# A token factor that moves behind the MLP's ReLU, one pass over the second half of the output projection, and seven-product up blocks throughout

## The chip, the cores and the metric

The kernel runs on one core of a Trainium2 chip. The metric is the device time of one execution in microseconds; the kernel before takes 2443.19 us as the median of three runs (2441.78 to 2445.8). In the text PE is TensorE, DVE is VectorE, ACT is ScalarE, POOL is GpSimd and SP is SyncE, which issues most of the DMAs.

## What is computed

One layer of a hybrid decoder for 512 prompt tokens and 8 x 4 sample tokens, so 544 columns, model width 2048, MLP width 8192. All of it is fp32. The part that matters here is the second half of the layer:

```
x = x + concat(y_conv, y_delta) @ w_out
h = x * rsqrt(mean(x * x, axis=-1) + EPS) * norm_ffn_w
x = x + square(relu(h @ w_up)) @ w_down
y = rms_norm(x, final_norm_w)
```

The norm has a weight for each of the 2048 features (`norm_ffn_w`) and a factor for each token (the rsqrt). The token factor is positive and the same for all features, so it can be multiplied in before the product with `w_up` or behind it and behind the ReLU.

## The kernel before

**Tiling.** Features lie on the 128 partitions, tokens on the free axis, as two token halves of 272 columns (256 prompt, 16 sample). `x2p` holds x as 8 pair tiles, each of 2 feature tiles by 2 token halves by 272. Every fp32 product is made of three reduced-precision (fp32r) matmuls on split operands: high weight by high x, high by low, low by high (`product`, and the inner loop of `bilinear`). A split is two instructions: ACT copies the value to the high part, DVE subtracts that from the value for the low part. For a weight tile that is `weight` (L142 on ACT, L145 on DVE, 1024 columns, behind a 512 KB load into one of two `w_raw` buffers); for an operand it is `parts_into` (L989 and L990). High and low weights have three buffers each, and `ahead` prepares weights two steps early.

**Output projection.** The first half, `first_part` over `w_o1`, makes both token halves with each weight, into a two-bank tile `ps_big`. The second half runs over `steps`, first all 16 feature tiles for token half 0, then all 16 for half 1. Each of the 16 `w_o2` weights is thus loaded and split twice and used for 24 matmuls each time, into `ps_small`. Each step adds the result into `x2` on DVE (L916), squares the sum on ACT (L1010), adds the square to `ssq` on POOL (L1014) and, after odd steps, stores half of a pair tile (L1016, POOL's queue). `rstd_rows` turns `ssq` into the token factor `r2`: a matmul with ones, Ln and Exp on ACT, one Newton step on DVE. `normalise` multiplies weight and factor into x (L1001, 32 DVE instructions).

**Up.** The 32 blocks of 256 hidden units are of two kinds. The first `N_PLAIN` = 3 are plain: for each token half, two outputs of two weights by 8 k by 3 matmuls, so 192 matmuls a block, each weight loaded once for each half. They end in a Relu on ACT (L1042) for each output. The other 29 are `Pair` blocks: 2x2 blocks of the weights by 2x2 blocks of x in seven products instead of eight, 7 by 8 k by 3 = 168 matmuls of 272 columns. Products run in `ORDER` = 1, 2, 6, 5, 7, 3, 4. The four weight quarters (`w_q`, a11 to a22) come by SP (L1107) into six buffers `g` and two buffers `xe`, the same space that `x2p` held; product 6 forms s1, a21, a11 and a12 on DVE (L1117 to L1120); then each of the seven is split (L1124 on ACT, L1125 on DVE). The x side of the products, tiles c0, c1, c4, d and their parts, is prepared while the plain blocks run.

**Behind a block.** `block_out` copies products 1, 6, 5 from PSUM on ACT (L1190), adds 2, 7, 3 on DVE (L1196), applies Relu to three quarters after product 3 (L1198, 816 wide) and to the last after 4 (L1192, out of PSUM), and squares all on ACT (L1193, 1088 wide). `keep_sums` forms the sums that the way down needs (L1072 to L1076), splits them (L989, L990) and stores them through POOL's queue (`ucd`). Blocks 0 and 1 are kept in another form (`u0_d`), 2 and 31 are stored as they are (`u_d`).

**Order.** The Tile scheduler orders each engine's instructions by priority; `urgent()` raises it. On an engine the instructions run in that order, and an instruction that waits holds all behind it.

Of the kernel before, what the change touches and what calls it, by code (L numbers as in the profile page):

```python
# [9 lines left out]
F32 = mybir.dt.float32  # L10
# [29 lines left out]
N_PLAIN = 3  # L40
# [17 lines left out]
def trunk(ctx, tc, a):  # L58
# [112 lines left out]
    def rstd_rows(out, ssqs, t, halves=(0, 1)):  # L171

        for h in halves:
            pr = ps_small(HT)
            for i, q in enumerate(ssqs):
                PE.matmul(pr, ones, q[:, h, :], start=i == 0, stop=i == len(ssqs) - 1)
            y, th = out[:, h, :], t[:, h, :]
# [772 lines left out]
    sqp = pool("sq", 2, late)  # L950
# [21 lines left out]
    u0_d = [tile_in(dram, f"u0d{m}", [P, 2, 2, 2, HT]) for m in KEPT]
    uc_d = {m: tile_in(dram, f"ucd{m}", [P, 14, HT]) for m in range(N_PLAIN, NF - 1)}
# [11 lines left out]
    def halves_of(t):  # L985
        return t[:, 0, :], t[:, 1, :]

    def parts_into(hi, lo, src):
        S.activation(hi, src, AF.Copy)  # L989
        V.tensor_tensor(lo, src, hi.bitcast(F32), SUB)  # L990


    ssq = t_tile("ssq2", "hi")[:, 0:2]
    r2 = r1
    N2 = KT - N1
    h_c = [{} for _ in range(KT // 2)]

    def normalise(i, h):
        for j in range(2):
            o = 2 * i + j  # L1000
            V.scalar_tensor_tensor(x2[o][:, h], x2[o][:, h], nv[:, KT + o : KT + o + 1], r2[:, h], MUL, MUL)  # L1001

    steps = [(h, o) for h in range(2) for o in range(KT)]
    for (h, ob), w in ahead(steps, lambda it: weight(a["w_o2"][it[1]], N2 * P)):
        ps = ps_small(HT)
        for k in range(N2):
            product({h: ps}, w, k * P, cat[N1 + k], k == 0, k == N2 - 1, (h,))
        add(x2[ob][:, h], ps)
        sq = tile_in(sqp, "sq", [P, HT])
        S.activation(sq, x2[ob][:, h], AF.Square)  # L1010
        if ob == 0:
            G.tensor_copy(ssq[:, h, :], sq)
        else:
            (G if ob < KT - 2 else V).tensor_tensor(ssq[:, h, :], ssq[:, h, :], sq, ADD)  # L1014
# [12 lines left out]

    d_c = [None] * (KT // 2)

    def plain(m, h):  # L1030
        t = t_tile("u", "u")
        u = t[:, :2]
        for i in range(2):
            ps = ps_small(HT)
            for j in range(2):
                with urgent():
                    w = weight(a["w_up"][m, 2 * i + j], 1024)
                for k in range(KT // 2):
                    x = h_c[k][1 + j] if h == 0 else (d_c[k][0][:, j], d_c[k][1][:, j])
                    product({h: ps}, w, k * P, tuple((t, t) for t in x), j == k == 0, j == 1 and k == 7, (h,))  # L1040
            with urgent():
                S.activation(u[:, i], ps, AF.Relu)  # L1042
        with urgent():
            S.activation(u, u, AF.Square)
        if m not in KEPT:
            for i in range(2):
                nc.gpsimd.dma_start(u_d[m][:, 2 * i + 1 - h], u[:, i])
            return
        hi = t[:, 2:4].bitcast(F32R)
        parts_into(hi, u.bitcast(F32R), u)  # L1050
        for i in range(2):
            nc.gpsimd.dma_start(u0_d[m][:, 0, i, h], t[:, 2 + i])
            nc.gpsimd.dma_start(u0_d[m][:, 1, i, h], u[:, i])

    plain(0, 0)
    with urgent():
        rstd_rows(r2, [ssq], t_tile("rt", "T")[:, 0:2], (1,))
    for m in range(1, N_PLAIN):
        plain(m, 0)
    for i in range(KT // 2):  # L1060
        normalise(i, 1)
        p = cmb if i < 7 else cmb2
        d_c[i] = c_tile(p, "d_hi"), c_tile(p, "d_lo")
        parts_into(*d_c[i], x2p[i][:, :, 1, :])
        h_c[i][3] = d_c[i][0][:, 1], d_c[i][1][:, 1]
    for m in range(N_PLAIN):
        plain(m, 1)


    def sums(t, b11, b12, b21, b22, third=True):  # L1070

        V.tensor_tensor(t[:, 1, :], b12, b11, SUB)  # L1072
# [5 lines left out]
    for i in range(KT // 2):
        t = t_tile("tc", ("T", "hi")[i % 2])
        sums(t, *(x2p[i][:, j, h, :] for j in range(2) for h in range(2)), third=False)  # L1080
        hi, lo = c_tile(hlp, "c1_hi"), c_tile(hlp, "c1_lo")
        parts_into(hi, lo, t[:, 0:2, :])
        h_c[i].update({6: (hi[:, 0], lo[:, 0]), 5: (hi[:, 1], lo[:, 1])})
        e = c_tile(cmb2, "c4")
        parts_into(e[:, 0], e[:, 1], t[:, 3, :])
        h_c[i][4] = e[:, 0], e[:, 1]
# [9 lines left out]
    class Pair:  # L1096
# [31 lines left out]
    def bilinear(items, early, cs, outs):  # L1128
# [15 lines left out]
        for (w, p), (whi, wlo) in ahead(items, load):  # L1144
# [39 lines left out]
    def block_out(m):  # L1184
        u = t_tile("u", "u")

        def out(p, ps):
            with urgent():
                if p in (1, 6, 5):
                    S.activation(u[:, {1: 1, 6: 0, 5: 2}[p]], ps, AF.Copy)  # L1190
                elif p == 4:
                    S.activation(u[:, 3], ps, AF.Relu)  # L1192
# [24 lines left out]
    KS = list(range(N_PLAIN, NF - 1))  # L1217
# [274 lines left out]
```

## Time and profile before

| | |
|---|---|
| median of 3 runs | 2443.19 us |
| the profiled execution's own time | 2444.58 us |
| its span in the trace | 2442.8 us |
| PE busy | 2388.2 us |
| DVE busy | 1807.5 us |
| ACT busy | 1080.9 us |
| POOL busy | 495.8 us |
| output projection, second half | 920.6 to about 1023.5 us |
| plain up blocks | to about 1105.6 us |
| seven-product up blocks | to about 1710 us |

The page of the profile gives for each engine the time in which it ran something. Of more use here is the trace by stages: a line of the timeline is start, duration, engine, source line, what is written from what, shape, and in brackets how long the engine had been idle before and what ended that. Differences between starts of the same kind of instruction give the pace of a stage.

### The profile page before, as it was taken

What the parts mean: (1) busy time and instruction counts of PE and PEld (TensorE: products, weight loads), DVE (VectorE), ACT (ScalarE), POOL (GpSimd) and SP (SyncE); (2) the same over time, 40 slices, a digit from 0 to 9 for tenths busy, and PEclk for the clock granted to TensorE, in tenths of its full rate; (3) what the DMA queues carried; (4) which work ended last, traced back from release to release, by engine and by line L of the source; (5) the groups of instructions that cost most, each with busy time, mean ns of one, the idle gap of its engine ahead of it and who ended that gap; (6) DMA issues with size and microseconds to landing.
All of it is one profiled execution on the core that took longest, in us unless ns stands there. A gap on an engine that the chain in (4) does not pass through costs nothing.

```text
span 2442.8 us, 47373 instructions
## 1 busy us (share of the span) xinstructions
PE 2388.2 (98%) x19089; PEld 2362.3 (97%) x19089; DVE 1807.5 (74%) x2937; ACT 1080.9 (44%) x1598; POOL 495.8 (20%) x776
## 2 busy tenths in 40 slices
PE   8999999999999999999999999999899999999997
PEld 8999999999999999998999999999899999999997
DVE  9675575666658535788888888887487788888885
ACT  6424332532432424565555555555233333333445
POOL 5123212312412304410010111110401212121003
PEclk9999999999999999999999999999999999999999
DMA  6233333332423546565555555556945646464433
GB/s 202 93 114 116 98 110 97 122 106 86 134 89 96 173 141 199 199 213 196 194 191 200 200 200 191 189 191 210 375 137 168 226 162 225 154 223 151 143 93 111
DMA packets 144275, 397.96 MB, mean 163 GB/s; under 512 B 35348, under 2 KB 44216, under 8 KB 144056
## 3 DMA queue, kind: packets, MB, share of 16 engines
q1 hardware_dynamic: 108648, 266.12, 34.3%
q0 software_dynamic: 35408, 128.82, 14.2%
q8 instruction: 150, 2.46, 0.4%
q14 instruction: 69, 0.57, 0.1%
HBM read 317.37 MB, written 77.49 MB: 162 GB/s over the span
## 4 chain that ended last, share of the span: by engine, by line
PE 83%; DVE 6%; DMA 6%; issue 2%; ACT 2%; SPq 0%; DVEq 0%; POOLq 0%; POOL 0%; ACTq 0%
PE ps_s L76 46%; PE ps_big L76 29%; PE ps_sm L76 8%; DVE w_lo L145 2%; DMA w_raw<-in_w_o_dram 2%; DMA w_q<-in_w_d_dram 1%; DMA w_raw<-in_w_up_dram 1%; ACT w_hi L142 1%; DVE w_lo L1125 1%; DMA w_q<-in_w_up_dram 1%; DVE x L1001 0%; PE ps_sm L80 0%; DVE yx L799 0%; DMA w_raw<-in_w_d_dram 0%; DMA ud<-u 0%
## 5 line engine op out<-in xcount | busy, mean ns | idle before, releaser
L1124 ACT ACTIVATE w_hi<-w_q 128x768 fp32r<-128x768 f32 (+3 forms) x422 | 375.4, 890 | 555.7 <-PE ps_s L76 496.1
L76 PE MATMUL ps_s<-uc,w_hi 128*128 128x272 f32 x3136 | 592.1, 288 | 5.3 <-DVE x2v L916 4.4
L76 PEld LDWEIGHTS ps_s<-uc,w_hi 128*128 128x128 f32 x3136 | 491.0, 188 | 7.9 <-issue 5.3
L1125 DVE TENSOR_TENSOR w_lo<-w_q,w_hi 128x768 fp32r<-128x768 f32 (+3 forms) x422 | 425.5, 1009 | 59.5 <-ACT w_hi L1124 58.0
L76 PE MATMUL ps_s<-uc,w_lo 128*128 128x272 f32 x1568 | 450.3, 288 | 0.0
L76 PE MATMUL ps_big<-x_hi,w_hi 128*128 128x272 f32 x2016 | 426.4, 293 | 1.3 <-ACT x_hi L157 1.1
L76 PE MATMUL ps_big<-x_hi,w_lo 128*128 128x272 f32 x2016 | 419.3, 289 | 2.6 <-DVE w_lo L145 2.6
L76 PE MATMUL ps_big<-x_lo,w_hi 128*128 128x272 f32 x2016 | 420.2, 289 | 0.3 <-DVE x_lo L160 0.3
L142 ACT ACTIVATE w_hi<-w_raw 128x1024 fp32r<-128x1024 f32 (+3 forms) x215 | 211.4, 983 | 454.0 <-PE ps_big L76 297.6
L145 DVE TENSOR_TENSOR w_lo<-w_raw,w_hi 128x1024 fp32r<-128x1024 f32 (+3 forms) x215 | 279.1, 1298 | 142.0 <-ACT w_hi L142 138.6
L76 PEld LDWEIGHTS ps_big<-x_hi,w_hi 128*128 128x128 f32 x2016 | 317.6, 189 | 5.8 <-ACT x_hi L157 2.3
L76 PEld LDWEIGHTS ps_big<-x_hi,w_lo 128*128 128x128 f32 x2016 | 316.4, 189 | 3.5 <-DVE w_lo L145 3.4
L76 PEld LDWEIGHTS ps_big<-x_lo,w_hi 128*128 128x128 f32 x2016 | 317.7, 189 | 0.7 <-DVE x_lo L160 0.5
L76 PEld LDWEIGHTS ps_s<-uc,w_lo 128*128 128x128 f32 x1568 | 295.0, 188 | 0.0
L76 PE MATMUL ps_s<-c_hi,w_hi 128*128 128x272 f32 x928 | 267.7, 288 | 4.8 <-ACT w_hi L1124 4.2
L76 PE MATMUL ps_s<-c_hi,w_lo 128*128 128x272 f32 x928 | 268.6, 289 | 1.2 <-DVE w_lo L145 0.7
L76 PE MATMUL ps_s<-c_lo,w_hi 128*128 128x272 f32 x928 | 267.6, 288 | 0.0
L1224 POOL DMA_DIRECT2D uc<-ucd x196 | 106.2, 547 | 437.2 <-PE ps_s L76 420.0
L916 DVE TENSOR_TENSOR x2v<-x2v,ps_s 128x272 f32<-128x272 f32 x326 | 140.2, 435 | 66.6 <-PE ps_s L76 64.6
L76 PEld LDWEIGHTS ps_s<-c_hi,w_hi 128*128 128x128 f32 x928 | 175.9, 189 | 5.3 <-ACT w_hi L1124 4.4
L76 PEld LDWEIGHTS ps_s<-c_hi,w_lo 128*128 128x128 f32 x928 | 175.5, 189 | 2.0 <-DVE w_lo L1125 1.0
L76 PEld LDWEIGHTS ps_s<-c_lo,w_hi 128*128 128x128 f32 x928 | 175.5, 189 | 0.0
(375 smaller groups left out, 4224.6 us busy)
## 6 DMA issues: line engine op xcount, KB each, us to landing
w_q<-in_w_up_dram SPq DMA_DIRECT2D x116, 512.0 KB, 4.8
w_raw<-in_w_in_dram SPq DMA_DIRECT2D x106, 512.0 KB, 3.3
uc<-ucd POOLq DMA_DIRECT2D x196, 272.0 KB, 5.7
w_q<-in_w_d_dram SPq DMA_DIRECT2D x128, 384.0 KB, 3.4
w_raw<-in_w_o_dram SPq DMA_DIRECT2D x32, 512.0 KB, 3.4
ucd<-u_hi POOLq DMA_DIRECT2D x28, 544.0 KB, 5.6
ucd<-tc POOLq DMA_DIRECT2D x28, 544.0 KB, 6.7
w_raw<-in_w_up_dram SPq DMA_DIRECT2D x28, 512.0 KB, 3.5
```

The lines of the kernel that those rows point to most:

```text
L76: return cls.held(nc.tensor.matmul(*args, **kw))
L142: S.activation(hi[:, c], raw[:, c], AF.Copy)
L145: V.tensor_tensor(lo[:, c], raw[:, c], hi[:, c].bitcast(F32), SUB)
L916: V.tensor_tensor(out, out, ps, ADD)
L1124: S.activation(hi, s, AF.Copy)
L1125: V.tensor_tensor(lo, s, hi.bitcast(F32), SUB)
L1224: nc.gpsimd.dma_start(t.bitcast(F32), uc_d[KS[j]][:, 2 * b : 2 * b + 2])
```

## The change

- The second half of the output projection runs once over the 16 `w_o2` weights, each with both token halves, 48 matmuls into `ps_big`. Squares, sums and the stores of x are 544 columns or whole pair tiles. The PSUM pool `small2` opens behind it.
- The norm's weight is multiplied in on ACT (`scaled`, 16 instructions kept in program order); the token factor no longer goes into x. `normalise` is gone.
- `operands` prepares c0, d and c4 of pair i-1 in place while the projection works on pair i. The c1 tiles follow behind the last pair, and with them the last readers of the `x2p` space that the quarters use.
- The plain blocks are gone: all 32 blocks take seven products. The first `N_EARLY` = 2 run products 1, 2, 4 of both blocks, with direct weight loads and product 4 in a bank of its own, then 6, 5, 7, 3 of each.
- The token factor is made for both halves after product 4 of block 0.
- `block_out` copies 1, 6, 5 and 4, adds 2, 7, 3, and then `done` runs one DVE instruction over 1088 columns, max with 0 and product with the token factor, ahead of the Square. Both Relus are gone.

```
-    steps = [(h, o) for h in range(2) for o in range(KT)]
-    for (h, ob), w in ahead(steps, lambda it: weight(a["w_o2"][it[1]], N2 * P)):
-        ps = ps_small(HT)
+    def scaled(i):
         for j in range(2):
             o = 2 * i + j
+            tc.keep_in_program_order(
+                S.activation(xs[i][:, j], x2p[i][:, j], AF.Copy, scale=nv[:, KT + o : KT + o + 1])
+            )
+    def operands(i):
+        x = xs[i]
+        b11, b12, b21, b22 = (x[:, j, h, :] for j in range(2) for h in range(2))
+        hi, lo = c_tile(hlp, "c0_hi"), c_tile(hlp, "c0_lo")
+        parts_into(hi, lo, x[:, :, 0, :])
...
+        V.tensor_tensor(b11, b12, b11, SUB)
+        V.tensor_tensor(b12, b22, b12, SUB)
+        V.tensor_tensor(b22, b22, b11, SUB)
+        V.tensor_tensor(b21, b21, b22, SUB)
...
+    for ob, w in ahead(range(KT), lambda o: weight(a["w_o2"][o], N2 * P)):
+        ps = ps_big()
         for k in range(N2):
-            product({h: ps}, w, k * P, cat[N1 + k], k == 0, k == N2 - 1, (h,))
-        add(x2[ob][:, h], ps)
+            product(ps[0], w, k * P, cat[N1 + k], k == 0, k == N2 - 1)
+        add(x2[ob], ps[1])
+        sq = t_tile("sq", "u")[:, 0:2]
+        S.activation(sq, x2[ob], AF.Square)
...
+            nc.gpsimd.dma_start(x2_d[i], x2p[i])
+            if i:
+                scaled(i - 1)
+                operands(i - 1)
     with urgent():
-        rstd_rows(r2, [ssq], t_tile("rt", "T")[:, 0:2], (1,))
...
+        scaled(KT // 2 - 1)
+        operands(KT // 2 - 1)
+        for i in (0, 2, 3, 4, 1, 5, 6, 7):
+            hi, lo = c_tile(hlp, "c1_hi"), c_tile(hlp, "c1_lo")
+            parts_into(hi, lo, xs[i].rearrange("p j h t -> p (j h) t")[:, 0::3])
+            h_c[i].update({5: (hi[:, 0], lo[:, 0]), 6: (hi[:, 1], lo[:, 1])})
...
+        def done():
+            with urgent():
+                V.scalar_tensor_tensor(
+                    u.rearrange("p (i s) t -> p i s t", s=2), u.rearrange("p (i s) t -> p i s t", s=2), 0.0,
+                    r2.unsqueeze(1).broadcast_to([P, 2, 2, HT]), MAX, MUL,
+                )
+                S.activation(u, u, AF.Square)
...
-                if p in (1, 6, 5):
-                    S.activation(u[:, {1: 1, 6: 0, 5: 2}[p]], ps, AF.Copy)
-                elif p == 4:
-                    S.activation(u[:, 3], ps, AF.Relu)
-                    S.activation(u, u, AF.Square)
+                if p in (1, 6, 5, 4):
+                    S.activation(u[:, {1: 1, 6: 0, 5: 2, 4: 3}[p]], ps, AF.Copy)
...
-                if p == 3:
-                    S.activation(u[:, 0:3], u[:, 0:3], AF.Relu)
...
+            if p == 4 and m == 0:
+                with urgent():
+                    rstd_rows(r2, [ssq], hi_t[:, 2:4], swap=True)
...
+    firsts, rest = ups[:N_EARLY], ups[N_EARLY:]
+    items = [(w, p) for w in firsts for p in (1, 2, 4)] + [(w, p) for w in firsts for p in (6, 5, 7, 3)]
+    items += [(w, p) for w in rest for p in ORDER]
+    bilinear(items, firsts, lambda m: h_c, block_out)
```

The diff gives no order of the engines' instructions; three places of it follow. DVE in one steady up block of the kernel before, from the first combination of the quarters (L1117) to the block's split of u; `w_s` is s1, `w_q` a quarter, `u` the block's result, `tc` its sums:

```order
L1117 TENSOR_TENSOR w_s_15654<-w_q 128x1024
L1125 TENSOR_TENSOR w_lo<-w_q,w_hi 128x1024
L1118 TENSOR_TENSOR w_q<-w_q 128x1024
L1120 TENSOR_TENSOR w_q<-w_q 128x1024
L1125 TENSOR_TENSOR w_lo<-w_q,w_hi 128x1024
L1072 TENSOR_TENSOR tc<-u 128x272
L1075 TENSOR_TENSOR tc<-u 128x272
L1073 TENSOR_TENSOR tc<-u,tc 128x272
L1125 TENSOR_TENSOR w_lo<-w_s_15417,w_hi 128x1024
```

The same engine and place in the changed kernel:

```order
L1080 TENSOR_TENSOR w_s_15572<-w_q 128x1024
L1088 TENSOR_TENSOR w_lo<-w_q,w_hi 128x1024
L1081 TENSOR_TENSOR w_q<-w_q 128x1024
L1083 TENSOR_TENSOR w_q<-w_q 128x1024
L1154 SCALAR_TENSOR_TENSOR u<-u,r_91 128x1088
L1088 TENSOR_TENSOR w_lo<-w_q,w_hi 128x1024
L1088 TENSOR_TENSOR w_lo<-w_s_15335,w_hi 128x1024
L1052 TENSOR_TENSOR tc<-u 128x272
```

One instruction of 1088 columns (L1154) now stands between the combinations and the next split, and the sums of u stand one split later; nothing else moved.

ACT at the head of the up stage in the changed kernel, from the last square of the output projection (`sq`); `x2_6`, `xs` are the last two pairs of x, `r1` the token factor:

```order
L1022 ACTIVATE sq_12154<-x2_7_10315 128x544
L994 ACTIVATE x2_6_10313<-x2_6_10313,nv_81 128x544 x2
L978 ACTIVATE c0_hi_12160<-x2_6_10313 128x544
L978 ACTIVATE d_hi_12164<-x2_6_10313 128x272 x2
L179 ACTIVATE r1_91<-ps_sm_12341,eps_t_83 128x272
L179 ACTIVATE r1_91<-ps_sm_12349,eps_t_83 128x272
L180 ACTIVATE r1_91<-r1_91 128x272 x2
L978 ACTIVATE c4_12174<-x2_6_10313 128x272
L994 ACTIVATE xs_11091<-x2_7_10315,nv_81 128x544 x2
L978 ACTIVATE c0_hi_12179<-xs_11091 128x544
L978 ACTIVATE d_hi_12183<-xs_11091 128x272
```

Before, the last pair's operands were split while plain blocks ran; now the scaling and split of the last two pairs, with the token factor's Ln and Exp between them, stand ahead of products 1, 2 and 4 of the first block, which read them.

DVE a little later in the changed kernel, from the split of the last direct weight (`w_lo`, L145) to the split for product 6 of block 0:

```order
L145 TENSOR_TENSOR w_lo_12359<-w_raw_12357,w_hi_12358 128x1024
L979 TENSOR_TENSOR c1_lo_12213<-x2_1_9900,c1_hi_12212 128x544
L979 TENSOR_TENSOR c4_12174<-x2_6_10313,c4_12174 128x272
L979 TENSOR_TENSOR c1_lo_12217<-x2_5_10311,c1_hi_12216 128x544
L1080 TENSOR_TENSOR w_s1_12406<-w_q_12392,w_q_12393 128x1024
L979 TENSOR_TENSOR c1_lo_12221<-x2_6_10313,c1_hi_12220 128x544
L1081 TENSOR_TENSOR w_q_12392<-w_q_12390,w_q_12392 128x1024
L979 TENSOR_TENSOR c1_lo_12225<-xs_11091,c1_hi_12224 128x544
L1082 TENSOR_TENSOR w_q_12390<-w_s1_12406,w_q_12390 128x1024
L1175 TENSOR_TENSOR u_12364<-u_12364,ps_s_12415 128x272
L1083 TENSOR_TENSOR w_q_12391<-w_q_12391,w_q_12390 128x1024
L1088 TENSOR_TENSOR w_lo_12412<-w_q_12390,w_hi_12411 128x1024
```

The c1 splits read the last of the space into which the first quarters are loaded, and they stand among the combinations that wait for those loads; in the kernel before the first combination (L1117 of block 3) stood behind all operand splits, with the plain blocks' matmuls beside them.

More of the change, by code (lines that the diff above doesn't have):

```diff
@@ L169, in product, with rstd_rows @@
                 PE.matmul(ps[h], wp[:, c : c + P], x, start=start and i == 0, stop=stop and i == 2)
-    def rstd_rows(out, ssqs, t, halves=(0, 1)):
+    def rstd_rows(out, ssqs, t, halves=(0, 1), swap=False):
         for h in halves:
@@ L969, in trunk @@
     x2 = [x2p[i // 2][:, i % 2] for i in range(KT)]
+    KS = [m for m in range(NF) if m not in KEPT + STORED]
     x2_d = [tile_in(dram, f"x2d{i}", [P, 2, 2, HT]) for i in range(KT // 2)]
     u_d = {m: tile_in(dram, f"ud{m}", [P, 4, HT]) for m in STORED}
[L972 to L973 removed]
+    u0_d = [tile_in(dram, f"u0d{m}", [P, 2, 4, HT]) for m in KEPT]
+    uc_d = {m: tile_in(dram, f"ucd{m}", [P, 14, HT]) for m in KS}
@@ L975, in trunk, with parts_into @@
     first_part(KT - 1, lambda: None)
     ln_exp(True)
+    def parts_into(hi, lo, src):
+        S.activation(hi, src, AF.Copy)
+        V.tensor_tensor(lo, src, hi.bitcast(F32), SUB)
+    hi_t = t_tile("ssq2", "hi")
+    ssq, r2 = hi_t[:, 0:2], r1
+    N2 = KT - N1
+    h_c = [{} for _ in range(KT // 2)]
+    xs = list(x2p)
+    xs[-1] = t_tile("xs", "T").rearrange("p (j h) t -> p j h t", j=2)
+    def scaled(i):
+        for j in range(2):
+            o = 2 * i + j
+            tc.keep_in_program_order(
+                S.activation(xs[i][:, j], x2p[i][:, j], AF.Copy, scale=nv[:, KT + o : KT + o + 1])
+            )
@@ L983, in bank @@
         return t[:, :HT]
[L985 to L1001, printed above, removed]
@@ L1028, in trunk @@
[L1028 to L1043, printed above, removed]
-            S.activation(u, u, AF.Square)
[L1045 to L1053, printed above, removed]
@@ L1055, in trunk, with sums @@
-    plain(0, 0)
-    with urgent():
-        rstd_rows(r2, [ssq], t_tile("rt", "T")[:, 0:2], (1,))
[L1058 to L1070, printed above, removed]
+    def sums(t, b11, b12, b21, b22):
@@ L1072, in sums @@
         V.tensor_tensor(t[:, 1, :], b12, b11, SUB)
         V.tensor_tensor(t[:, 0, :], b22, t[:, 1, :], SUB)
-        if third:
-            V.tensor_tensor(t[:, 2, :], b22, b12, SUB)
+        V.tensor_tensor(t[:, 2, :], b22, b12, SUB)
         V.tensor_tensor(t[:, 3, :], b21, t[:, 0, :], SUB)
[L1078 to L1086, printed above, removed]
@@ L1110, in parts @@
             n = self.n
-            if p in (1, 2) and self.q is None:
-                return weight(self.src[p - 1], n)
+            if p in (1, 2, 4) and self.q is None:
+                return weight(self.src[{1: 0, 2: 1, 4: 3}[p]], n)
             a11, a12, a21, a22 = self.q
@@ L1149, in bilinear @@
                 w.ps, w.out = {"x": bank(True)}, outs(w.key)
-            if p in (2, 5):
-                w.ps["y" if p == 2 else "z"] = bank(False)
-            ps = w.ps[{2: "y", 5: "z", 3: "z"}.get(p, "x")]
+            alone = p == 4 and w in early
+            if p in (2, 5) or alone:
+                w.ps["z" if p == 5 else "y"] = bank(False)
+            ps = w.ps["y" if alone else {2: "y", 5: "z", 3: "z"}.get(p, "x")]
             c = cs(w.key)
```

78 lines of the change are left out of this document (36 added, 42 removed).

## Prediction

> **What bounds the kernel now.** I read first the busy times and the chain of work that ended last, then windows by stage, then the timelines at the seams of the stages.
>
> ```profile
> PE 2388.2 (98%) x19089; PEld 2362.3 (97%) x19089; DVE 1807.5 (74%) x2937; ACT 1080.9 (44%) x1598; POOL 495.8 (20%) x776
> PE 83%; DVE 6%; DMA 6%; issue 2%; ACT 2%; SPq 0%; DVEq 0%; POOLq 0%; POOL 0%; ACTq 0%
> ```
>
> PE is busy for 98% of the span and holds 83% of the chain. So time is won by fewer matmuls, or where PE waits. The windows (stretch, length, then busy time of PE, its weight loads, DVE, ACT and POOL, granted clock, DMA share, GB/s) show where it waits:
>
> ```profile
> 920.50:1018.00 97.50, 94.82 (x748) 93.40 (x747) 65.84 (x91) 46.93 (x69) 47.22 (x41) 1.00 0.62 203
> 1027.00:1119.00 92.00, 82.87 (x629) 79.63 (x628) 73.52 (x120) 52.57 (x85) 10.71 (x20) 0.99 0.65 214
> 1119.00:1710.00 591.00, 590.50 (x4695) 589.63 (x4695) 493.28 (x560) 341.47 (x419) 60.07 (x111) 1.00 0.56 195
> ```
>
> The 591 us of seven-product blocks leave PE idle for 0.5 us; the plain stretch leaves it idle for 9.1 of 92 us. The up stage can thus gain nothing by shorter work on DVE or ACT, and only loses once they become later than PE. The pace of each stage comes from these starts (DVE's adds, then ACT's copies of the last plain output and of three blocks' last products):
>
> ```profile
> 914.52 0.72 DVE L916 TENSOR_TENSOR x<-x,ps_big 128x544 f32<-128x544 f32 x1 [1.94 <-PE ps_big L76]
> 920.60 0.72 DVE L916 TENSOR_TENSOR x<-x,ps_big 128x544 f32<-128x544 f32 x1 [0.98 <-PE ps_big L76]
> 923.59 0.44 DVE L916 TENSOR_TENSOR x<-x,ps_sm 128x272 f32<-128x272 f32 x1 [0.92 <-PE ps_sm L76]
> 1023.46 0.43 DVE L916 TENSOR_TENSOR x<-x,ps_sm 128x272 f32<-128x272 f32 x1
> 1105.60 0.38 ACT L1042 ACTIVATE u<-ps_sm 128x272 f32<-128x272 f32 x1
> 1173.92 0.38 ACT L1192 ACTIVATE u<-ps_s 128x272 f32<-128x272 f32 x1
> 1194.95 0.38 ACT L1192 ACTIVATE u<-ps_s 128x272 f32<-128x272 f32 x1
> 1215.97 0.38 ACT L1192 ACTIVATE u<-ps_s 128x272 f32<-128x272 f32 x1
> ```
>
> 48 matmuls with both halves per weight take 6.08 us, 24 with one half 2.99, a block of 168 takes 21.02 (0.1251 us a matmul). From the end of the first half of the projection (920.60) to the end of the third seven-product block (1173.92) pass 253.3 us. PE's work in it: 32 x 2.985 = 95.5 for the second half, 576 x 0.1251 = 72.1 for the plain blocks, 3 x 21.02 = 63.1, 0.9 for the ones matmuls; 231.6 in all. So 21.7 us there are loss: 102.9 instead of 95.5 to 1023.46, 82.1 instead of 72.1 to 1105.60, 68.3 instead of 63.1 after it. One piece of that can be seen alone, at the first product that needs combined quarters:
>
> ```profile
> 1118.33 0.59 PE L76 MATMUL ps_s<-c_hi,w_hi 128*128 128x272 f32 x1 [4.18 <-ACT w_hi L1124]
> 1119.60:1122.00 2.40, 2.36 (x10) 2.36 (x11) 2.40 (x3) 0.57 (x1) 0.00 (x0) 0.50 0.56 167
> 1124.00:1126.00 2.00, 2.00 (x15) 2.00 (x14) 0.70 (x2) 1.20 (x2) 0.00 (x0) 0.82 0.46 184
> ```
>
> PE stood still for 4.18 us, and behind it the granted clock was 0.50: 10 matmuls in 2.4 us, 0.24 us each instead of 0.125. Full speed is back within the second of these windows, about 5.4 us after the wait's end; I put the cost of it at 2.4 us.
>
> **The change, part by part.**
>
> *Matmuls.* The plain blocks' 576 become 3 x 168 = 504: 72 x 0.1251 = **9.0 us less**. The second half of the projection goes from 95.5 to 16 x 6.08 = 97.3: 1.8 more.
>
> *The waits in their place.* In the projection PE needs a new weight every 6.08 us instead of every 2.99, and DVE has less to do:
>
> ```profile
> L145 DVE TENSOR_TENSOR w_lo<-w_raw,w_hi 128x1024 fp32r<-128x1024 f32 x58 | 72.6, 1251 | 48.6 <-ACT w_hi L142 48.2
> L990 DVE TENSOR_TENSOR c_lo<-tc,c_hi 128x544 fp32r<-128x544 f32 x8 | 5.8, 720 | 0.0
> L1072 DVE TENSOR_TENSOR tc<-x 128x272 f32<-128x272 f32 x8 | 3.5, 439 | 0.0
> L1014 POOL TENSOR_TENSOR ssq<-ssq,sq 128x272 f32<-128x272 f32 x26 | 37.3, 1436 | 28.2 <-ACT sq L1010 28.1
> ```
>
> For each pair of outputs (12.16 us): 2 x 1.25 for w_lo, 2 x 0.72 for the adds, 0.72 for c0, and seven instructions of 272 columns (two d_lo, four combinations, c4) at 0.44: 7.7 us, 64%. I count no loss. The scaling on ACT waits for the store of x that it overwrites, one pair (12.16 us) later; that is off the path.
>
> Behind the projection (T0) six direct products come, 18.0 us, and 0.9 of ones matmuls. By the order on ACT, the last pair's scaling stands behind Ln and Exp, and these behind the ones matmuls. At 0.65 us for 544 and 0.43 for 272 columns (estimates after DVE's rows of these widths) c0 of the last pair is about 1.2 us late; its low part costs 0.8, smaller ones 0.3. Eight c1_lo (0.72) between the direct w_lo (1.25) make those of block 1 late by 1.7 and 1.2. Loss 5.2: PE wants product 6 of block 0 at T0 + 24.1.
>
> The quarters for it land in space that the c1 splits still read, until T0 + 18.5 by the same tally. Their load and the combinations:
>
> ```profile
> w_q<-in_w_up_dram SPq DMA_DIRECT2D x116, 512.0 KB, 4.8
> 1106.16 7.04 DMA w_q<-in_w_up_dram
> 1192.88 1.23 DVE L1117 TENSOR_TENSOR w_s<-w_q 128x1024 f32<-128x1024 f32 x1 [1.04 <-DMA w_q<-in_w_up_dram]
> ```
>
> 18.5 + 4.8 + three combinations of 1.22 + two c1_lo of 0.72 + 1.06 for w_hi = T0 + 29.5; with the 7.04 of the first load before, 31.7. So a wait of 4.18 us goes and one of 5.4 (to 7.6) comes at the same kind of place, with half clock behind it, 2.4. Losses 5.2 + 5.4 + 2.4 = 13.0, and 0.9 for the last copy's delay at the seams.
>
> Sum to the end of the sixth block: 97.3 + 6 x 21.02 + 0.9 + 13.0 + 0.9 = 238.2 instead of 253.3, **15.1 less**.
>
> The Trainium skill ("TensorE: Matmul & The Clock Gate", section "HAM oscillation — how this bites in real kernels") says that PE gaps over about 3.4 us bring the clock down to half. This trace agrees (4.18 us, then 0.50). By that rule a gap of 3 us here would cost no 2.4 on top; that is the better rival below.
>
> *The instruction behind the ReLU.* 32 times 128x1088 on DVE. ACT loses its two Relus a block; at 341 busy us of 591 in the stage this frees nothing on the path. The trace has no such shape, but these:
>
> ```profile
> L1001 DVE SCALAR_TENSOR_TENSOR x<-x,nv,r 128x272 f32<-128x272 f32 x32 | 16.1, 538 | 0.0
> L504 DVE SCALAR_TENSOR_TENSOR tmp<-tmp,nv 128x544 f32<-128x544 f32 x8 | 6.3, 783 | 8.4 <-ACT tmp L502 8.3
> L160 DVE SCALAR_TENSOR_TENSOR x_lo<-xr,nv,x_hi 128x544 fp32r<-128x544 f32 x16 | 20.3, 1291 | 2.7 <-ACT x_hi L157 2.7
> 1224.40 1.28 DVE L990 TENSOR_TENSOR tc<-tc,u_hi 128x1088 fp32r<-128x1088 f32 x1
> ```
>
> By the first two, 0.538 + 3 x 0.245 = 1.27; the last, two tensors of the same width, took 1.28; by L160 twice 1.291 = 2.58. I take 1.27, nearest in width; below nothing is excluded on DVE, since nothing there goes away in a block. Whether it is hidden depends on a loop, one quarter's buffer:
>
> ```profile
> 1186.03 1.22 DVE L1125 TENSOR_TENSOR w_lo<-w_q,w_hi 128x1024 fp32r<-128x1024 f32 x1 [0.66 <-ACT w_hi L1124]
> 1194.02 1.22 DVE L1125 TENSOR_TENSOR w_lo<-w_q,w_hi 128x1024 fp32r<-128x1024 f32 x1
> 1219.33 0.44 DVE L1072 TENSOR_TENSOR tc<-u 128x272 f32<-128x272 f32 x1
> 1221.99 1.01 DVE L990 TENSOR_TENSOR u<-u,u_hi 128x816 fp32r<-128x816 f32 x1
> ```
>
> The last w_lo of a block ends at 1187.25, the load into that buffer lands at 1192.88 (5.63), and DVE, which runs in order, takes the next s1. From s1 to the next block's last w_lo DVE runs, at the pace of back-to-back starts (1194.02 - 1192.88 = 1.14): nine instructions of 1024 columns, 10.2; four sums and an add at 0.35, 1.75; 0.92 and 1.2 for the splits of u: 14.1. Loop 14.1 + 5.63 = 19.7 us against PE's 21.02: slack 1.3. With 1.27 more it is **21.0: hidden, with nothing left**. That cover was also what absorbed the waits for stores:
>
> ```profile
> ACT u_hi L989 <- DMA ucd<-u_hi: 16.0, 8, 3.4
> ```
>
> Eight delays, 2 us each in the mean. If each cost what is over the lost slack in the worst order it would be some 10 us; I take 2. The stores and sums of the new blocks 0 to 2 replace plain ones; the way down is the same (0, plus or minus 1).
>
> **Sum.** 2444.6 (the profiled execution's own time, 1.4 above the median of 2443.19) - 15.1 + 2 = 2431.5, **2431**. Its own range is 2427 to 2437.
>
> **Rivals.**
>
> *Better, 2421 to 2427.* The c1 splits end early enough that PE's gap before product 6 stays short: 5.4 - 3 = 2.4 less, 2.4 of half clock less, and the small waits of 5.2 partly hidden. For it: ACT has slack. Against it: ACT is in order and stands behind Ln. 2431 - 4.8 - 2 = 2424.
>
> *DVE late in the projection, about 2438.* POOL's adds may hold DVE up:
>
> ```profile
> 1000.38 2.13 DVE L145 TENSOR_TENSOR w_lo<-w_raw,w_hi 128x1024 fp32r<-128x1024 f32 x1
> 1000.54 0.88 POOL L1014 TENSOR_TENSOR ssq<-ssq,sq 128x272 f32<-128x272 f32 x1
> ```
>
> This w_lo took 0.9 us more than its mates, beside an add of 0.88. The adds at 544 columns, twice 1.436 each by the group's mean, 14 of them: 40 us. If they exclude DVE wholly, 8 x 7.7 + 40 = 102 of 97.3, with uneven ends about 7 us late: 2431 + 7 = 2438. By the 0.88 it fits (25 + 62 = 87). The skill ("SBUF — State Buffer", section "SBUF: two separate sides") calls the port pair of DVE and GpSimd an exclusive lock, held for a whole instruction; the row agrees, and by that rule this rival has its 102.
>
> *Slower: the new instruction makes the loop longer than PE's block.* At 2.58 us the loop is 14.1 + 5.63 + 2.58 = 22.3, so 1.3 over 21.02 in each of 28 blocks, 36 us: 2444.6 - 15.1 + 36 = 2465. It eats the whole gain from 15.1 / 28 = 0.54 a block, which is an instruction of 1.8 us, or 0.55 us more on the quarter's load. For it: the slack is gone by my own sum, and stores delay u_hi. Against: DVE's 493 us of 591 plus 28 x 1.27 is 529, 89%, and the wider row of 1.28.
>
> That the plain matmuls, Relus or `normalise` remain somewhere is excluded by the order.
>
> **Chances.** Forecast 0.53, better 0.12, DVE late in the projection 0.15, slower 0.13 (of it 0.03 with a loss that just cancels the gain), the rest 0.07 smaller mishaps from 2437 up, 0.02 of it over 2448. The range 2421 to 2446 leaves out the slower rival and the best corner. About 0.2% (5 us) is what a measurement of this kernel can tell from no change: faster than 2438.3 is the forecast, the better case and a part of the projection's: 0.71; within, 0.17; slower, 0.12.
>
> **What would show it.** Right: the adds of the second half every 6.08 us; one wait of 5 us or so before the first product 6, with the clock at 0.50 behind it; p4's copies 21.02 apart in the up stage; the new instruction near 1.27 us. Wrong: copies 21.3 or more apart with PE waiting for w_lo or w_hi behind s1; adds of the projection over 6.3 apart; the new instruction beyond 1.8 us.

## The result and the profile after

The changed kernel takes 2471.31 us (median of 4 runs, 2468.61 to 2474.9) against 2444.49 us before (4 runs): 1.1% slower, ratio 1.0112, 95% interval 1.0093 to 1.0130. The prediction of 2431, with 2421 to 2446 as its range, was wrong.

The page of the changed kernel, the chain that ended last and its costliest lines:

```profile
PE 77%; DVE 8%; DMA 8%; issue 4%; ACT 2%; SPq 0%; DVEq 0%; POOL 0%; POOLq 0%; ACTq 0%
PE ps_s L76 38%; PE ps_big L76 33%; PE ps_sm L76 6%; DMA w_q<-in_w_up_dram 6%; DVE w_lo L1088 2%; DVE u L1154 1%; ACT w_hi L1087 1%; DVE w_lo L145 1%; DVE w_q L1081 1%; DMA w_q<-in_w_d_dram 1%; DVE w_q L1083 1%; ACT u L1172 1%; DMA w_raw<-in_w_in_dram 0%; PE ps_sm L80 0%; DVE yx L799 0%
```

PE's share of the chain fell from 83% to 77%, and the load of the up weights' quarters, 1% before, holds 6%. Where the span's 24.0 us more (2466.8 against 2442.8) arose is read from the Squares on ACT, one for each block. Before, blocks 5, 30 and 31:

```profile
1174.33 1.12 ACT L1193 ACTIVATE u<-u 128x1088 f32<-128x1088 f32 x1
1700.63 1.12 ACT L1193 ACTIVATE u<-u 128x1088 f32<-128x1088 f32 x1
1726.79 1.11 ACT L1193 ACTIVATE u<-u 128x1088 f32<-128x1088 f32 x1
```

After, blocks 3, 4, 5, 30 and 31:

```profile
1118.13 1.10 ACT L1158 ACTIVATE u<-u 128x1088 f32<-128x1088 f32 x1
1142.01 1.11 ACT L1158 ACTIVATE u<-u 128x1088 f32<-128x1088 f32 x1 [2.78 <-DVE u L1154]
1164.47 1.11 ACT L1158 ACTIVATE u<-u 128x1088 f32<-128x1088 f32 x1 [1.65 <-DVE u L1154]
...
1729.51 1.10 ACT L1158 ACTIVATE u<-u 128x1088 f32<-128x1088 f32 x1
1755.90 1.11 ACT L1158 ACTIVATE u<-u 128x1088 f32<-128x1088 f32 x1 [2.21 <-DVE u L1154]
```

| stretch | before | after | difference |
|---|---|---|---|
| start to block 5's Square | 1174.3 | 1164.5 | -9.9 |
| block 5 to block 30 | 526.3 (21.05 a block) | 565.0 (22.60 a block) | +38.7 |
| block 30 to 31 | 26.2 | 26.4 | +0.2 |
| block 31 to the end | 716.0 | 710.9 | -5.1 |

The whole loss is in the steady up stage: blocks come every 22.6 us instead of 21.05. It starts with block 4 (1118.13 to 1142.01); up to block 3 the kernel was ahead. The windows show the same for 400 us out of that stage (1200 to 1600; busy time of each engine), first of the kernel before, then of the changed one:

```profile
sum 400.00, PE 399.98 PEld 399.27 DVE 334.60 ACT 232.84 POOL 41.15; mean PE 399.98 PEld 399.27 DVE 334.60 ACT 232.84 POOL 41.15
```

```profile
sum 400.00, PE 377.72 PEld 373.51 DVE 335.31 ACT 202.37 POOL 37.89; mean PE 377.72 PEld 373.51 DVE 335.31 ACT 202.37 POOL 37.89
```

PE now stands still for 22 of 400 us. DVE is busy for 335 us as before, with an instruction more in each block but only some 17.7 blocks in the 400 us instead of 19. It is idle for 65 of the 400 us, so DVE's work isn't the bound either: both wait for something. The waits of the whole run say who waited, for whom, in total, how often, longest:

```profile
PE ps_s L76 <- ACT u L1172: 36.5, 29, 1.9
```

That is PE, 29 times, at a product for ACT's copy of product 1. The chain in the middle of the stage (start, length, what; links under 0.1 us and those called issue left out) tells why the copy is late:

```profile
1188.58 6.17 PE ps_s L76 x47
...
1194.77 1.07 ACT w_hi L1087
...
1195.87 1.24 DVE w_lo L1088
...
1197.12 6.27 DMA w_q<-in_w_up_dram
...
1204.63 1.22 DVE w_lo L1088
1205.85 1.08 DVE w_q L1081
...
1208.03 1.30 DVE u L1154
...
1210.37 0.39 ACT u L1172
...
1210.80 6.17 PE ps_s L76 x47
```

From 1188.58 to 1210.80 it is a ring, a chain of waits that comes back to its own start one block later, of 22.2 us: PE's products 6 and 5 (6.17) free a high-weight buffer; ACT and DVE split product 4's weight; with that split the buffer of the last quarter is free and the block after next loads into it (6.27); DVE's s1 needs that load, and DVE runs in order, so the split and the two combinations behind s1, and then the new instruction (L1154), wait with it; ACT's Square waits for the new instruction, the copy of product 1 stands behind the Square on ACT, and PE's next product 6 waits for the copy. The new instruction itself takes what was forecast:

```profile
L1154 DVE SCALAR_TENSOR_TENSOR u<-u,r 128x1088 f32<-128x1088 f32 x32 | 41.1, 1284 | 0.0
```

### The profile page after: what moved, and what is told of

Same layout as the page of the kernel before. It is cut to its first block, busy times and chain, and to the rows that moved or that the text cites. A ratio compares the mean times of both kernels' runs of the same rounds, so it can differ in the third digit from the quotient of the medians.

```text
span 2466.8 us, 46994 instructions
## 1 busy us (share of the span) xinstructions
PE 2387.5 (97%) x19017; PEld 2359.0 (96%) x19017; DVE 1827.1 (74%) x2921; ACT 1044.1 (42%) x1545; POOL 466.5 (19%) x739
## 4 chain that ended last, share of the span: by engine, by line
PE 77%; DVE 8%; DMA 8%; issue 4%; ACT 2%; SPq 0%; DVEq 0%; POOL 0%; POOLq 0%; ACTq 0%
PE ps_s L76 38%; PE ps_big L76 33%; PE ps_sm L76 6%; DMA w_q<-in_w_up_dram 6%; DVE w_lo L1088 2%; DVE u L1154 1%; ACT w_hi L1087 1%; DVE w_lo L145 1%; DVE w_q L1081 1%; DMA w_q<-in_w_d_dram 1%; DVE w_q L1083 1%; ACT u L1172 1%; DMA w_raw<-in_w_in_dram 0%; PE ps_sm L80 0%; DVE yx L799 0%
## 5 line engine op out<-in xcount | busy, mean ns | idle before, releaser
L76 PE MATMUL ps_big<-x_hi,w_hi 128*128 128x272 f32 x2272 | 479.4, 292 | 1.1 <-ACT w_hi L142 0.8
L76 PE MATMUL ps_big<-x_hi,w_lo 128*128 128x272 f32 x2272 | 472.3, 289 | 2.4 <-DVE w_lo L145 2.4
L76 PE MATMUL ps_big<-x_lo,w_hi 128*128 128x272 f32 x2272 | 473.6, 289 | 0.0
L76 PEld LDWEIGHTS ps_big<-x_hi,w_hi 128*128 128x128 f32 x2272 | 357.9, 189 | 5.5 <-issue 1.4
L76 PEld LDWEIGHTS ps_big<-x_hi,w_lo 128*128 128x128 f32 x2272 | 356.7, 188 | 3.3 <-DVE w_lo L145 3.2
L76 PEld LDWEIGHTS ps_big<-x_lo,w_hi 128*128 128x128 f32 x2272 | 358.1, 189 | 0.2
L142 ACT ACTIVATE w_hi<-w_raw 128x1024 fp32r<-128x1024 f32 (+3 forms) x177 | 171.2, 967 | 415.6 <-PE ps_big L76 338.2
L76 PE MATMUL ps_s<-c_hi,w_hi 128*128 128x272 f32 x1024 | 299.1, 292 | 37.4 <-ACT u L1172 32.4
L145 DVE TENSOR_TENSOR w_lo<-w_raw,w_hi 128x1024 fp32r<-128x1024 f32 (+3 forms) x177 | 230.5, 1303 | 94.7 <-ACT w_hi L142 89.4
L76 PE MATMUL ps_s<-c_lo,w_hi 128*128 128x272 f32 x1024 | 295.9, 289 | 0.2 <-DVE c_lo L979 0.2
L916 DVE TENSOR_TENSOR x2v<-x2v,ps_s 128x272 f32<-128x272 f32 x326 | 139.9, 434 | 67.1 <-PE ps_s L76 65.3
```

The costliest lines, as they stand in the source:

```text
L76: return cls.held(nc.tensor.matmul(*args, **kw))
L142: S.activation(hi[:, c], raw[:, c], AF.Copy)
L145: V.tensor_tensor(lo[:, c], raw[:, c], hi[:, c].bitcast(F32), SUB)
L916: V.tensor_tensor(out, out, ps, ADD)
```

## The experiments

Theory A: the ring over the quarter's load sets the pace; the new instruction made it longer than PE's 21.02 us, by its place more than by its length. Theory B: each block got longer by DVE's 1.28 us, wherever they stand. All kernels are the changed kernel with the edit shown.

**1. Square behind the copy** (`square_behind_copy`)

```
+                if 2 <= m < NF - 1:
+                    later.append((u, rest))
+                    return
                 S.activation(u, u, AF.Square)
...
+                    if p == 1 and later:
+                        u_last, rest_last = later.pop()
+                        with tc.issue_after(copied.ins):
+                            S.activation(u_last, u_last, AF.Square)
```

> Only the order on ACT is changed: from block 2 on, the Square of a block stands behind the next block's copy of product 1, so that copy no longer waits for the token-factor instruction. Theory A (a ring: PE's products 6 and 5 release the high-weight buffer, ACT and DVE split product 4's weight, the quarter is loaded into its buffer, DVE runs s1 and what stands ahead of the token-factor instruction, ACT's Square, the copy, PE's product 6 again; 22.5 us in the changed kernel): the ring is open, the wait of product 6 for the copy goes. What is left is DVE's own ring, 15.3 us of DVE and a load of 5.6 to 6.5, so 21.0 to 21.8 us a block; 2429 to 2450 us. Theory B (the 1.28 us that each block costs DVE more are what the blocks got longer by, wherever they stand): no change, 22.5 us a block, 2471 us.

Measured: 2474.55 us, ratio 1.0128 (1.0102 to 1.0153). Theory A's forecast was a miss. PE's wait for the copy is gone, but another has its size:

```profile
PE ps_s L76 <- DVE w_lo L1088: 30.6, 29, 1.4
```

On DVE's timeline (the first and the last split of a block's round, and s1):

```profile
1310.90 1.22 DVE L1088 TENSOR_TENSOR w_lo<-w_q,w_hi 128x1024 fp32r<-128x1024 f32 x1
...
1318.21 1.23 DVE L1080 TENSOR_TENSOR w_s<-w_q 128x1024 f32<-128x1024 f32 x1 [2.49 <-DMA w_q<-in_w_up_dram]
```

The last w_lo ends at 1312.12 and s1 starts 6.1 us later, after a wait of 2.49 us. So there are two rings through the same load, one over PE and ACT and one on DVE alone, and the second isn't shorter: 6.1 us of load, and 16.4 of 22.5 us from s1 (1295.75) to the last w_lo, with 0.76 us of a wait for u_hi in it. Opening the first won nothing: the loss does not hang on the wait for the copy.

**2. The token-factor instruction ahead of s1** (`factor_ahead_of_s1`)

```
+    factor = {}
+    def behind(key):
+        ins = factor.get(key - 2) if isinstance(key, int) else None
+        return nullcontext() if ins is None else tc.issue_after(ins.ins)
...
-                    V.tensor_tensor(self.s1, a21, a22, ADD)
-                    V.tensor_tensor(a21, a11, a21, SUB)
+                    with behind(self.key):
+                        V.tensor_tensor(self.s1, a21, a22, ADD)
+                        V.tensor_tensor(a21, a11, a21, SUB)
...
-                V.scalar_tensor_tensor(
+                factor[m] = V.scalar_tensor_tensor(
```

> Only the order on DVE is changed: s1 and a21 of the block after next, which wait for the quarter's load, stand behind the token-factor instruction instead of ahead of it. Theory A: the load leaves the ring, the token-factor instruction runs as soon as product 4 is copied, blocks come every 21.02 us and PE's waits for the copy go; about 2430 us, below the kernel before. Theory B (length of DVE's work): no change, 22.5 us a block, 2471 us. A third, C (the quarters' loads got slower, 6.3 us against 5.6, and that is the cause): between, 21.7 us, about 2450.

Measured: 2429.4 us, ratio 0.9941 (0.9920 to 0.9962): 42 us less than the changed kernel, and faster than the kernel before. DVE's timeline has the instruction, s1 behind it without a wait:

```profile
1329.51 1.28 DVE L1161 SCALAR_TENSOR_TENSOR u<-u,r 128x1088 f32<-128x1088 f32 x1
1330.71 1.22 DVE L1087 TENSOR_TENSOR w_s<-w_q 128x1024 f32<-128x1024 f32 x1
```

The split that frees the quarter's buffer ended at 1320.92, so 9.8 us lie between it and s1, and DVE fills them with work that needs no load. The windows of 400 us:

```profile
sum 400.00, PE 400.00 PEld 400.00 DVE 363.41 ACT 213.25 POOL 41.24; mean PE 400.00 PEld 400.00 DVE 363.41 ACT 213.25 POOL 41.24
```

PE never stands still, with DVE busy for 363 of 400 us. DVE does in this kernel exactly what it does in the changed one; theory B is refuted. So is C: from 1200 to 1600 us a quarter takes up to 8.5 us to land here (8.4 in the changed kernel), and nothing waits for it. s1 here belongs to the block after next and is not needed for some 20 us: it was its place in DVE's order that made others wait for its load.

**3. No token factor** (`no_factor`). The token factor is left out and the Relus run on ACT as before.

```
-                V.scalar_tensor_tensor(
-                    ...
-                    r2.unsqueeze(1).broadcast_to([P, 2, 2, HT]), MAX, MUL,
-                )
...
+                    if p == 3 and not first:
+                        S.activation(u[:, 0:3], u[:, 0:3], AF.Relu)
```

> The token factor is left out of the MLP and the Relus run on ACT as in the kernel before; all else is as in the changed kernel. Prices the rest of the change. All theories: 21.02 us a block; the parts ahead of block 2 gave 14 us against the kernel before in the trace, so 2430 us. If it is not below 2440, the loss lies elsewhere than in the new instruction.

Measured: 2432.23 us, ratio 0.9949 (0.9932 to 0.9966). The rest of the change is worth some 12 us, and the loss comes with the new instruction. s1 still waits for its load here, 23.1 us in 19 waits within the 400 us (21.6 in 18 before, 36.3 in 18 in the changed kernel), but PE is busy for 400.00 of them: with that much less on DVE the ring closes in time.

**4. Both orders** (`both_orders`): the edits of 1 and 2 together.

> Both edits of order together. Theory A: 21.02 us a block as with the second alone, 2430 us, nothing more. If the edits add up, each cut only a part of the loss. Theory B: 2471 us.

Measured: 2429.11 us, ratio 0.9939 (0.9918 to 0.9960), as with the second alone.

**5. The factor on half of each block** (`half_factor`): max and factor on two quarters only, left out of the others.

```
-                    u.rearrange("p (i s) t -> p i s t", s=2), u.rearrange("p (i s) t -> p i s t", s=2), 0.0,
-                    r2.unsqueeze(1).broadcast_to([P, 2, 2, HT]), MAX, MUL,
+                V.scalar_tensor_tensor(u[:, 0:2], u[:, 0:2], 0.0, r2, MAX, MUL)
```

> Max with 0 and token factor are applied to two of the four quarters of each block, 544 columns instead of 1088, and left out of the other two; by the order on DVE the instruction also stands one combination earlier. Theory A (ring on DVE: 15.7 us of DVE from s1 to the last w_lo, 0.8 of a wait for u_hi, 6.1 to 6.5 of the quarter's load, 22.5 us): 0.6 us less in the ring, 21.9 us a block, which is still over 21.02: about 27 x 0.6 = 16 us less than the changed kernel, 2455 us. If the place ahead of one combination had been what counts (the ring over ACT's copy, 1.1 us shorter too): 21.02 and about 2430.

Measured: 2471.22 us (2 runs), ratio 1.0109 (1.0090 to 1.0129): no change at all. Both numbers of theory A missed; a ring of fixed lengths is refuted as well. DVE's part from s1 to the last w_lo did fall, to 15.0 us (1319.52 to 1334.53) from 15.8 in the changed kernel. What took the place of what was saved is the load:

```profile
1310.09 1.22 DVE L1088 TENSOR_TENSOR w_lo<-w_q,w_hi 128x1024 fp32r<-128x1024 f32 x1
...
1319.52 1.23 DVE L1080 TENSOR_TENSOR w_s<-w_q 128x1024 f32<-128x1024 f32 x1 [3.62 <-DMA w_q<-in_w_up_dram]
```

8.2 us from the end of the w_lo (1311.31) to s1. In this stretch the DMA engines (share before the last number) have no room:

```profile
1308.00:1310.00 2.00, 2.00 (x18) 2.00 (x18) 1.90 (x2) 1.91 (x3) 1.03 (x2) 1.00 0.93 331
1310.00:1312.00 2.00, 2.00 (x18) 2.00 (x18) 1.31 (x2) 0.32 (x3) 0.54 (x1) 1.00 0.96 240
1312.00:1314.00 2.00, 2.00 (x19) 2.00 (x18) 1.38 (x2) 1.03 (x1) 0.00 (x0) 1.00 0.94 376
1314.00:1316.00 2.00, 2.00 (x19) 2.00 (x18) 1.86 (x3) 1.06 (x1) 0.00 (x0) 1.00 1.04 384
```

SP issued three quarters at 1306.76, 1308.81 and 1311.33, and POOL three of the block's four stores beside them, at 1307.94, 1309.14 and 1310.47. Three times 512 KB and 408 + 544 + 544 KB, 3.1 MB, at some 330 GB/s (the mean of these rows) take 9 us, and the quarter on which the ring closes is among the last of it. In the changed kernel it is the same picture, milder: three stores at 1193.60, 1194.79 and 1196.12, so 3.5 to 1.0 us ahead of the last quarter (1197.12); DMA share 0.95 from 1194 to 1197; load 6.3 us. Before, the stores came at 1180.38, 1183.21 and 1184.53, 6.9 to 2.8 us ahead of the last quarter (1187.28), and its load took 5.6. The engines were no freer there (0.97 and 0.98 from 1185 to 1189), but the stores had a longer lead.

**6. Fewer bytes stored** (`half_stores`): stores hold the high parts and one of seven low parts; the way down reads high parts in place of the low ones.

```
             nc.gpsimd.dma_start(d[:, at : at + n], hi.bitcast(F32))
-            nc.gpsimd.dma_start(d[:, 7 + at : 7 + at + n], src)
+            if at == 0:
+                nc.gpsimd.dma_start(d[:, 7:8], src[:, 0:1])
...
-            nc.gpsimd.dma_start(t.bitcast(F32), uc_d[KS[j]][:, 2 * b : 2 * b + 2])
+            nc.gpsimd.dma_start(t.bitcast(F32), uc_d[KS[j]][:, 2 * (b % 4) : 2 * (b % 4) + 2])
```

> The changed kernel, but of what each up block stores for the way down, the low parts are left out except one of seven (1088 KB a block instead of 1904), and the way down reads high parts in their place, as many bytes as before. All instructions on PE, ACT and DVE and their order are those of the changed kernel. Theory A (the ring closes over the quarter's load, and that load takes 6 to 8 us because the last three quarters of a block and three of its four stores pass the DMA engines together, busy share 0.93 to 1.04): the load falls to about 4 us, the ring to 20.5, blocks come every 21.02 us, about 2432 us. Theory B (DVE's 1.28 us more a block): DVE does the same work in the same order, 22.5 us a block, 2471 us. If it lies between, the load is part of the ring, but not by that contention alone.

Measured: 2431.41 us (6 runs), ratio 0.9949 (0.9933 to 0.9965), as theory A has it. With the engines' instructions and their order as in the changed kernel, the quarters land after 4.9 us at most (8.4 in the changed kernel, from 1200 to 1600 us), s1 waits 2.4 us in all, and PE is busy throughout:

```profile
sum 400.00, PE 400.00 PEld 399.84 DVE 359.49 ACT 214.86 POOL 30.75; mean PE 400.00 PEld 399.84 DVE 359.49 ACT 214.86 POOL 30.75
```

So the contention of stores and quarters is a necessary part of the loss, as is the place of the new instruction. Neither makes the loss alone: in experiment 2 the stores come as close to the last quarter (1317.56, 1318.76 and 1320.08, against 1320.95), the DMA share is 0.96 from 1321 to 1324, and PE waits for nothing. That the new instruction itself pushes the stores into the loads (it holds u back, the stores follow u) agrees with experiment 3: without it the stores are 5.8 to 3.1 us ahead of the last quarter again (1311.13, 1312.32 and 1313.81, against 1316.91), and over the rounds from 1200 to 1600 us s1 starts 5.7 us behind the w_lo that frees its buffer in the median, against 6.6 in the changed kernel and 5.6 before. Whether it is the bytes or the number of the stores that counts (three instead of four a block in experiment 6) was not tried.

**7. The order of 2, and the token factor's Ln later** (`order_and_late_rstd`)

```
             S.activation(y, pr, AF.Ln, bias=eps_t, scale=1.0 / D)
+            if pin:
+                tc.keep_in_program_order(ln)
```

> The order on DVE with the token-factor instruction ahead of s1, and besides Ln of the token factor pinned on ACT behind the copy of block 0's product 4, so that the last pair's scaling no longer stands behind Ln, Exp and the ones matmuls. In the changed kernel PE has four waits of 0.2 to 1.2 us within 4 us there, and behind them 6 us at a granted clock of 0.50. Theory A: scaling comes some 2 us earlier, these waits and that stretch of half clock (3 us) go, product 6 then waits 2 us longer for the quarters: 3 to 5 us less than with the order alone, 2425 us. Rival: the quarters' loads set the time of product 6 whatever stands ahead, half clock follows there, and nothing is won: 2429 us.

Measured: 2429.4 us (6 runs, 2425.8 to 2437.1), ratio 0.9941 (0.9927 to 0.9956). Nothing is won, as the rival had it, but not for its reason. PE's wait for product 6, and the wait of the high-weight copy that ended it:

```profile
1046.47 0.59 PE L76 MATMUL ps_s<-c_hi,w_hi 128*128 128x272 f32 x1 [5.90 <-ACT w_hi L1096]
1045.36 1.06 ACT L1096 ACTIVATE w_hi<-w_q 128x1024 fp32r<-128x1024 f32 x1 [4.36 <-DVE w_q L1091]
```

PE comes to product 6 some 3.0 us earlier than with the order alone (23.6 us behind the projection's last add instead of 26.6) and waits 5.90 us there instead of 2.57. It waits for DVE, not for the quarters: DVE's only wait from 1028 to 1048 is 1.51 us for a high weight (L142), and from 1035.98 on it runs without a gap, s1 at 1041.28 included. Seven short instructions of the token factor (L183 to L186, 2.2 us), which the later Ln moved there, now stand on DVE among the splits and combinations ahead of product 6.

## Why the prediction was wrong, point by point

**Paces and the projection: right.** The additions of the second half come every 6.08 us, and PE is without a gap there:

```profile
919.46 0.72 DVE L916 TENSOR_TENSOR x<-x,ps_big 128x544 f32<-128x544 f32 x1 [0.98 <-PE ps_big L76]
925.54 0.72 DVE L916 TENSOR_TENSOR x<-x,ps_big 128x544 f32<-128x544 f32 x1 [4.02 <-PE ps_big L76]
...
1016.74 0.72 DVE L916 TENSOR_TENSOR x<-x,ps_big 128x544 f32<-128x544 f32 x1 [2.74 <-PE ps_big L76]
```

97.28 us from the first of these rows to the last; 97.3 was the term. The rival that POOL's adds hold DVE up cost no time, but its mechanism is there. The 13 adds took 1357 to 1744 ns each, 20.4 us in all where the rival had 40, and beside them the low-weight splits took the same time each (shortest, median, longest in ns):

```profile
L145 DVE TENSOR_TENSOR w_lo<-w_raw,w_hi x15: 1218/1224/1227, 926.4 to 1011.8; 128x1024 fp32r<-128x1024 f32 x15
```

Five of the six c4 splits in the stretch, 272 columns, were held up, though: they took 1.60 us, and the sixth, with no add beside it, 0.43.

```profile
951.98 1.46 POOL L1026 TENSOR_TENSOR ssq<-ssq,sq 128x544 f32<-128x544 f32 x1 [4.92 <-ACT sq L1022]
952.14 1.60 DVE L979 TENSOR_TENSOR c<-x,c 128x272 fp32r<-128x272 f32 x1
```

Each of the five ends 0.3 us behind the add beside it. One c0 split beside another add took 2.02 us instead of 0.73. So the exclusive lock of the Trainium skill ("SBUF — State Buffer", section "SBUF: two separate sides"), by which that rival had its 102 us, agrees with these rows, though the low-weight splits show nothing of it. It took some 7 us from DVE, which was busy for only 59 of the 98 us, and the additions kept their pace.

**The seam into the up stage: right in sum, wrong in its parts.** Product 6 of block 0 was forecast for T0 + 29.5 and started at 1045.89, T0 + 29.15 (T0 = 1016.74). That the sum came out is luck. PE reached it 2.5 us later than forecast, so its wait is 2.56 us and not 5.4, and the half clock came earlier, behind four small waits:

```profile
1026.81 0.52 PE L76 MATMUL ps_s<-c_hi,w_hi 128*128 128x272 f32 x2 [1.24 <-ACT c_hi L978]
1027.57 0.39 PE L76 MATMUL ps_s<-c_lo,w_hi 128*128 128x272 f32 x1 [0.24 <-DVE c_lo L979]
1029.11 0.54 PE L76 MATMUL ps_s<-c_hi,w_hi 128*128 128x272 f32 x1 [0.77 <-ACT w_hi L142]
1030.40 0.59 PE L76 MATMUL ps_s<-c_hi,w_lo 128*128 128x272 f32 x1 [0.52 <-DVE w_lo L145]
1045.89 0.40 PE L76 MATMUL ps_s<-c_hi,w_hi 128*128 128x272 f32 x1 [2.56 <-ACT w_hi L1087]
1044.78 1.06 ACT L1087 ACTIVATE w_hi<-w_q 128x1024 fp32r<-128x1024 f32 x1 [1.02 <-DVE w_q L1082]
```

And the path was another. The forecast led over the quarters' load, 4.8 us behind the c1 splits. No instruction on DVE waits for that load here: from 1037.16 to 1048 DVE runs without a gap, s1 at 1039.93 included, and product 6 waits for DVE's own row of splits and combinations. One reading of the prediction was short as well: in the kernel before, full clock was back some 6.4 us behind the wait's end (matmuls are 0.13 us apart again from 1124.77), not 5.4.

The gain forecast for the parts ahead of the steady stage, 15.1 us, was there. Ahead of the first slow block the changed kernel copies product 4 of block 3 at 1115.13, 195.7 us behind the add at 919.46; the forecast gives 238.2 - 2 x 21.02 = 196.2. In experiment 2, where the stage runs at 21.00, product 4 of block 5 is copied 239.0 us behind the add (921.22 to 1160.24) instead of 253.3 before: 14.3 less.

**The instruction behind the ReLU: its price right, its cover wrong.** The step that failed is "With 1.27 more it is 21.0: hidden, with nothing left". Its 1.27 us was right (1.284). The ring's other two terms weren't. Two rounds of it in the changed kernel, each from the w_lo that frees the buffer to the s1 that waits for the load:

```profile
1195.87 1.23 DVE L1088 TENSOR_TENSOR w_lo<-w_q,w_hi 128x1024 fp32r<-128x1024 f32 x1
1203.48 1.23 DVE L1080 TENSOR_TENSOR w_s<-w_q 128x1024 f32<-128x1024 f32 x1 [1.72 <-DMA w_q<-in_w_up_dram]
...
1218.09 1.23 DVE L1088 TENSOR_TENSOR w_lo<-w_q,w_hi 128x1024 fp32r<-128x1024 f32 x1
1225.95 1.23 DVE L1080 TENSOR_TENSOR w_s<-w_q 128x1024 f32<-128x1024 f32 x1 [1.96 <-DMA w_q<-in_w_up_dram]
```

DVE's part from s1 to the end of the last w_lo was put at 14.1 + 1.27 = 15.4; here it is 15.8 (1203.48 to 1219.32), the same instructions with small gaps between them. The load was put at 5.63, taken from one row and held fixed; in the same way it is 6.4 and 6.6 here, 6.1 in experiment 1 and 8.2 in experiment 5. 15.8 + 6.6 makes the 22.5 us from one s1 to the next, instead of 21.0. Over all rounds from 1200 to 1600 us the medians are 15.8 and 6.6. The 5.63 was a fair middle value of the kernel before (median 5.6), but there too single rounds in which s1 waited lay between 4.8 and 7.1. The prediction's sum left a margin of 0.02 us in 21, and it priced what might break it as eight waits for stores, 2 us in all, instead of as 28 blocks times whatever the ring exceeds. The ring over PE, ACT's Square and the copy was not seen at all; it turned out no longer than the other.

**The slower rival had the place and one of its two conditions.** "0.55 us more on the quarter's load" was named as one way to lose the whole gain, and the load is 0.8 to 1.0 us longer in the changed kernel, with 0.4 us more on DVE. That its price of 36 us was close (38.7) is luck: it was worked out on an instruction of 2.58 us. Its chance of 0.13 came from arguing over the instruction's length, while the profile's own rows already showed s1 waiting for the load in the kernel before (1.04 us in the row of 1192.88).

**The way down: 0, plus or minus 1, was forecast, and it is 5.1 us shorter** from block 31's Square, 2.2 us of it because that Square comes later behind the new instruction (2.58 us behind the copy of product 4, instead of 0.41). Of the rest the waits show that PE waited 3.3 us once for the residual's first sum (L916) at that seam, where it waited 6.5 before; why the residual was there earlier was not tried.

## What to carry to other kernels

A load into a reused buffer closes a ring. Add it up over every engine that stands in it, in the order in which each runs, and treat the load's time as a variable: when the ring's work shifts, its own stores can meet its loads, and a margin of a few hundredths is none. Before shortening an added instruction look at what stands ahead of it in its engine's order: here the same instruction, with a load-dependent one that wasn't needed for 20 us (and the one behind that) moved behind it, turned a loss of 27 us into a gain of 14. And where halving a suspected cost changes nothing, look for something elastic in the ring; here it was a load that shares the DMA engines with the stores.

## What was not expected of the hardware

The granted clock fell to half without any long stop of PE. Around the four waits of 0.24 to 1.24 us shown above:

```profile
1026.00:1028.00 2.00, 0.95 (x5) 0.73 (x6) 2.00 (x6) 1.59 (x5) 0.00 (x0) 1.00 0.48 113
1028.00:1030.00 2.00, 1.10 (x5) 0.56 (x3) 2.00 (x4) 2.00 (x4) 0.00 (x0) 0.80 0.52 176
1030.00:1032.00 2.00, 1.60 (x7) 1.61 (x8) 2.00 (x6) 2.00 (x5) 0.00 (x0) 0.50 0.93 270
1032.00:1034.00 2.00, 2.00 (x11) 2.00 (x11) 2.00 (x5) 0.56 (x2) 0.00 (x0) 0.50 0.70 242
1034.00:1036.00 2.00, 2.00 (x10) 2.00 (x10) 1.14 (x2) 0.21 (x1) 0.00 (x0) 0.50 1.01 367
```

PE was busy for half of the 4 us from 1026 to 1030, the granted clock (third number from the end) went to 0.50 by 1030 and stayed there to 1036, and 10 matmuls took 2 us from 1034 on. Behind the single stop of 2.56 us that ended at 1045.89 it fell again, to 0.57 from 1046 to 1048. The Trainium skill's rule ("TensorE: Matmul & The Clock Gate", section "HAM oscillation — how this bites in real kernels") speaks of gaps over about 3.4 us; these rows don't agree with it as a threshold on one gap. The prediction's better rival, which hoped for full clock behind a stop of 3 us, would not have had it: 2.56 us was enough.
